# No-operations ahead of VectorE's first operation, and implied waits between an engine's own operations declared away, in a sum of reciprocals

## The chip, the cores and the metric

The kernel runs on one core of one Trainium2 chip. A core has five engines with instruction queues of their own: TensorE (PE in the profile; its weight loads are PEld), VectorE (DVE), ScalarE (ACT), GpSimd (POOL) and SyncE (SP), which here only issues DMAs. Sixteen DMA engines move data between HBM and the on-chip memory SBUF; TensorE writes to a second memory, PSUM, of eight banks. The metric is device time in microseconds (us) on the one core. One execution was profiled; durations and waits below are from it.

## The reference

```python
def setup_inputs():
    batch, seq, dim = 32, 512, 1024
    return {"x": np.abs(np.random.randn(batch, seq, dim)).astype(np.float32) + 1e-6}

def reference(x):
    return np.sum(1.0 / x, axis=-1).astype(np.float32)
```

The input is 32 x 512 rows of 1024 positive float32 numbers, 67.1 MB in all; the output is one sum of reciprocals per row. Nothing is reused, so every byte is read from HBM once.

## The kernel before

**Tiling.** Each of the 128 partitions holds 128 input rows ("row r" is one row in every partition, 128 x 1024 numbers). Rows arrive in `ring`, 40 row slots in SBUF. The last two rows are worked in two halves each, so they appear in the plan as 126 to 129.

**Arithmetic.** With a row's halves a and b, 1/a + 1/b = (a + b) / (a b). The product a*b is made by POOL (step P, line 199) or, for some rows, by DVE (V with one half copied into PSUM by a TensorE step C, line 209; W straight from SBUF; both line 220). ACT turns products into reciprocals in two passes, Ln (step L, line 242) and Exp with scale -1 (step E, line 251), usually two rows at once, in the `prod` slots or into PSUM. For some rows PE adds the halves into PSUM (step S, line 232, two matmuls with the identity `ident`). DVE ends every row with one multiply-and-accumulate (step R, line 267): over the whole row times the reciprocal, or over the added halves times the reciprocal. The profile shows it as a CUSTOM operation and a short READ_ACCUMULATOR that writes `sums`. A row's ring slot is free again after its last reader.

**Order of the work.** Nothing is scheduled automatically. `PLAN` is a list of tokens written out by hand (`P18`, `L16+2@18`, `R15`, `D9`); the loop over `ops` emits one instruction after the other, and each engine runs its own in that order. A `D` token issues the next loads on SP's DMA queue: 33 loads, first of 2, 10, 14 and 14 rows, later smaller, at the end one row and then half a row each. The results leave in six parts after the rows below 114 are done (line 289) and one at the end (line 291).

**Waits.** The framework puts a semaphore wait wherever an instruction touches a region that another one touched, unless it has already waited for a later instruction of that engine. `note` (line 135) keeps a history of who touched which ring half, `prod` slot or PSUM bank; for each operation of another engine that a wait already made is known to cover, it declares that there is no dependence, and the framework leaves the wait out. Pairs on the same engine are skipped by `if o_engine == engine: continue` (line 147), so for them the framework's waits stay. In the instruction list of this kernel that leaves 77 waits of ACT on its own semaphore, 21 of DVE and 17 of POOL. An instruction carries one wait; a further one becomes an instruction of its own ahead of it (EVENT_SEMAPHORE in the trace, not counted as busy): DVE has 45 of those among its 332 instructions, POOL 39.

Of the kernel before, what the change touches and what calls it, by code (L numbers as in the profile page):

```python
# [11 lines left out]
def kernel(  # L12
# [5 lines left out]
    nc = tc.nc  # L18
# [5 lines left out]
    R = 40  # L24
    NP = 22
    LAST = F - 2
    DONE = 114
    S = float(2**17)

    PLAN = """
        D2 D10 D14 D14 P0+2 C3@3 S2@0 V3 P2 L0+2@0 C11@3 S3@1 E0+2@6 P4+2 V11 L2+2@2 R0 S6@2
        E2+2 R1 P6+2 L4+2@4 R2 R3 E4+2@6 S7@0 P8+2 L6+2@8 R4 S10@1 E6+2 R5 P10 L8+2@10 R6 R7  # L40
        S11@2 E8+2@6 L10+2@6 R8 E10+2 R9 D11 R10 R11 P12+2 C19@3 S14@0 V19 P14+2 L12+2@12
        S15@1 E12+2@6 S18@2 R12 P16+2 L14+2@16 R13 E14+2 R14 P18 L16+2@18 R15 S19@0 E16+2@6
        P20+2 L18+2@14 R16 S22@1 E18+2 R17 D9 P22+2 L20+2@20 R18 R19 E20+2@6 S23@2 P24+2
        L22+2@0 R20 E22+2 R21 L24+2@2 R22 R23 E24+2@6 P26 C27@3 R24 S26@0 P28+2 V27 R25 D7
        L26+2@4 C35@3 E26+2 S27@1 P30+2 V35 L28+2@8 R26 S30@2 R27 E28+2@6 P32+2 L30+2@10 R28
        S31@0 E30+2 R29 P34 L32+2@12 S34@1 R30 R31 E32+2@6 P36+2 S35@0 L34+2@6 R32 E34+2 R33
        D7 P38+2 S38@2 L36+2@16 R34 R35 E36+2@6 S39@1 P40+2 L38+2@18 R36 C43@3 E38+2 R37 D6
        S42@0 P42 L40+2@14 V43 R38 E40+2@6 P44+2 R39 S43@2 L42+2@20 R40 E42+2 S46@1 R41 D3
        P46+2 L44+2@0 R42 R43 E44+2@6 S47@0 P48+2 L46+2@2 R44 S50@2 E46+2 R45 P50 L48+2@4
        R46 C51@3 R47 E48+2@6 S51@1 P52+2 V51 R48 D6 L50+2@8 C59@3 E50+2 R49 P54+2 S54@0  # L50
        L52+2@10 V59 R50 E52+2@6 R51 S55@2 P56+2 L54+2@12 R52 E54+2 S58@1 R53 D5 P58
        L56+2@16 R54 R55 E56+2@6 S59@0 P60+2 L58+2@6 R56 S62@2 E58+2 R57 D4 P62+2 L60+2@14
        R58 R59 E60+2@6 S63@1 P64+2 L62+2@18 R60 S66@0 E62+2 R61 D4 P66 L64+2@20 R62 C67@3
        R63 E64+2@6 P68+2 S67@2 V67 R64 L66+2@0 S70@1 R65 D4 E66+2 P70+2 L68+2@2 R66 R67
        S71@0 E68+2@6 P72+2 L70+2@4 R68 D3 E70+2 R69 D2 C75@3 P74 L72+2@10 S74@2 R70 V75
        P76+2 E72+2@6 R71 S75@1 L74+2@8 R72 D2 E74+2 R73 D2 P80 S78@0 L76+2@12 R74 P81
        L80@16 R75 S79@2 E76+2@6 P78+2 L81@17 R76 D2 S81@1 E80@5 E81 R80 L78+2@6 W82 E78+2
        R81 R77 D1 D1 D1 D1 D1 P88 C85@6 S85@1 R78 P83 L88@18 V85 E88@7 R79 P84 S84@0
        L82+2@14 R88 E82+2@5 P86+2 L84+2@19 R82 D1 E84+2 R83 D1 D1 D1 C90@7 P91 L86+2@0
        S91@2 R85 P93 V90 E86+2@5 R84 P92 S90@1 L90+2@2 R87 L93@21 W89 L92@10 R86 D1 D1 D1  # L60
        D1 E93@7 P94 S97@0 E92@6 R93 E90+2 P97 S94@3 L89@11 R92 E89@7 P95 L97@8 R91 S95@4
        E97 R90 L94+2@4 W96 R97 P101 C99@6 L96@9 R89 E94+2 S100@0 P98 V99 E96@5 L101@12 R95
        P100 S99@1 L98@13 R96 E101@7 L99+2@16 R101 E98@6 P104 C103@5 R94 E99+2 S105@2 R98
        P102 L104@18 V103 E104@7 W105 L102+2@6 R100 P107+2 C106@6 L105@14 R104 E102+2@4
        S108@0 V106 E105 R102 L106+3@19 P109 S107@3 R103 P110 E106+3 R105 S106@4 R99 P111+2
        L109+2@0 R107 S112@1 R108 E109+2@6 R106 L111+2@10 P114 R109 S111@0 E111+2 R110 P113
        L114@15 R111 C115@7 P116 L113@2 R112 E114@6 V115 E113@5 S117@0 P117 R114 L116@3
        L115@8 P118 E116@7 R113 S118@1 E115@6 P119 L117+2@12 R116 E117+2 R115 P120 S120@2
        L119@9 R117 P121 L120@4 S121@3 R118 E119@7 E120 R119 P122 L121@5 S122@0 E121 R120
        P123 L122@18 R121 E122 W124 L123@6 R122 L124@7 W125 S125@1 E123@7 E124@6 R123 P126  # L70
        L125@14 P127 L126@16 S127@0 R124 E125 P128 L127@17 S128@2 E126@7 P129 R125 E127
        S129@3 L128@19 R126 L129@20 E128 R127 E129 R128 R129
    """.split()

    Ln = mybir.ActivationFunctionType.Ln
    Exp = mybir.ActivationFunctionType.Exp
# [36 lines left out]
    def place(r):  # L113
        if r < LAST:
            return r, 0, H
        part, q = divmod(r - LAST, F - LAST)
        return LAST + q, part * H, H // 2
# [6 lines left out]
    left = set(range(DONE))  # L124
    bank, copied, halves, summed = {}, {}, set(), set()

    history = {}
    begun = {}
    count = {}
# [1 line left out]
    def note(engine, inst, reads=(), writes=()):  # L135
        inst = inst.ins
        known = dict(begun.get(engine, {}))
        before = {}
        for spaces, writing in ((reads, False), (writes, True)):
            for space in spaces:  # L140
                for other in history.get(space, ()):
                    if writing or other[3]:
                        before[other[0].name] = other
        needed = sorted(before.values(), key=lambda o: -o[4])
        for other in needed:
            o_inst, o_engine, o_tick, _, _, o_known = other
            if o_engine == engine:
                continue
            if o_tick <= known.get(o_engine, 0):
                tc.declare_no_dep(inst, o_inst, reason="implied by other waits")  # L150
                continue
            for e, t in o_known.items():
                known[e] = max(known.get(e, 0), t)
            known[o_engine] = max(known.get(o_engine, 0), o_tick)
        count[engine] = count.get(engine, 0) + 1
        begun[engine] = known
        entry = (engine, count[engine])
        if engine == "SP":
            entry = (f"load {count[engine]}", 1)
        for spaces, writing in ((reads, False), (writes, True)):  # L160
            for space in spaces:
                history.setdefault(space, []).append(
                    (inst, *entry, writing, sum(count.values()), known)
                )
# [10 lines left out]
    def slots(r, n):  # L175
        return [("slot", pslot[q]) for q in range(r, r + n)]

    with tc.manual_schedule():
        for op, r, n, b in ops:
            p = pslot.get(r)  # L180
# [59 lines left out]
            elif op == "L":  # L240
                pg = prod[:, p : p + n, : place(r)[2]]
                inst = nc.scalar.activation(out=pg, in_=pg, func=Ln, scale=S)  # L242
                note("ACT", inst, writes=slots(r, n))
            elif op == "E":
                pg = prod[:, p : p + n, : place(r)[2]]
                rc = pg
                if b is not None:
                    rc = ps[:, b : b + n, : place(r)[2]]
                    for j in range(n):
                        bank[r + j] = b + j  # L250
                inst = nc.scalar.activation(out=rc, in_=pg, func=Exp, scale=-1.0)  # L251
                if b is None:
                    note("ACT", inst, writes=slots(r, n))
                else:
                    banks = [("bank", b + j) for j in range(n)]
                    note("ACT", inst, slots(r, n), banks)
            elif op == "R":
                q, at, w = place(r)
                other = ps[:, bank[r], :w]
                if r in halves:  # L260
                    row = prod[:, p, :w]
                else:
                    row = ring[:, q % R, at : at + 2 * w]
                    row = row.rearrange("p (h e) -> p h e", h=2)
                    other = other.unsqueeze(1).to_broadcast([P, 2, w])
                total = sums[:, q : q + 1]
                inst = nc.vector.tensor_tensor_reduce(  # L267
                    out=row,
                    in0=row,
                    in1=other,  # L270
                    scale=S,
                    scalar=total if q in summed else 0.0,
                    op0=mult,
                    op1=add,
                    accum_out=total,
                )
                summed.add(q)
                note(
                    "DVE",
                    inst,  # L280
                    [("bank", bank[r])],
                    slots(r, 1) if r in halves else rows(r, 1),
                )

                left.discard(r)
                if not left:
                    for c in range(0, DONE, DONE // 6):
                        part = slice(c, min(c + DONE // 6, DONE))
                        nc.sync.dma_start(out=out_v[:, part], in_=sums[:, part])
                    left.add(-1)  # L290
        nc.sync.dma_start(out=out_v[:, DONE:], in_=sums[:, DONE:])


# [28 lines left out]
```

## Time and profile before

| | |
|---|---|
| time, median of 3 runs | 168.35 us (168.28 to 168.44) |
| the profiled execution: span from first to last instruction | 166.3 us |
| its own device time | not on the page; the median stands 2.05 us above its span |
| busy PE / DVE / ACT / POOL | 132.5 / 128.3 / 132.3 / 128.2 us |
| DMA, mean over the span | 404 GB/s, 67.26 MB |
| first load issued | 0.74 us |
| first operation of DVE | 19.89 us |
| last data operation of DVE starts | 163.95 us |

How to read it: the four computing engines are each busy some 130 of 166 us, so none is full over the whole span; the shares say nothing about a stage. The DMA line of the slices is the mean busy share of the sixteen DMA engines. Queue q1 carries the loads and stores; q8 and q14, marked "instruction", carry the engines' own program code. Waits name the engine or transfer that came last.

### The profile page before, as it was taken

The numbers are of one execution on the slowest core, as the hardware profiler recorded it, in microseconds if no ns is written. First come the engines' busy times: TensorE is split into PE (matmuls) and PEld (weight loads), VectorE is DVE, ScalarE is ACT, GpSimd is POOL, SyncE is SP. The second block draws the span as 40 slices with busy tenths as digits, with TensorE's granted clock in tenths as the row PEclk, the third lists the DMA queues.
The fourth block names the chain that finished last, engine by engine and source line by source line (L and its number), as shares of the span: only waits on it lengthen the run. The fifth ranks groups of instructions, "written<-read, shape, count | busy, mean of one in ns | idle before, by whom it ended". The sixth has DMA issues, their size and how long they took to land.

```text
span 166.3 us, 1348 instructions
## 1 busy us (share of the span) xinstructions
PE 132.5 (80%) x292; PEld 55.2 (33%) x292; DVE 128.3 (77%) x282; ACT 132.3 (80%) x157; POOL 128.2 (77%) x81
## 2 busy tenths in 40 slices
PE   0000799978855999999999999988699979989982
PEld 0000333333312444444343433324234424433351
DVE  0000119885787699898998898989899999999994
ACT  3040073949995899999799999996999999999992
POOL 1500795069995999999999999948977869999860
PEclk9999999999996999999999999999999999999999
DMA  5999999999998989999999999999999999999940
GB/s 189 536 394 394 441 441 441 441 441 441 441 441 349 509 368 446 430 417 438 441 434 434 406 426 446 429 424 424 414 437 437 414 410 428 410 409 410 400 139 4
DMA packets 5768, 67.26 MB, mean 404 GB/s; under 512 B 1536, under 2 KB 1536, under 8 KB 3200
## 3 DMA queue, kind: packets, MB, share of 16 engines
q1 hardware_dynamic: 5760, 67.18, 95.6%
q8 instruction: 2, 0.03, 0.1%
q14 instruction: 6, 0.05, 0.1%
HBM read 67.11 MB, written 0.07 MB: 404 GB/s over the span
## 4 chain that ended last, share of the span: by engine, by line
DMA 57%; PE 18%; ACT 8%; DVE 6%; POOL 6%; issue 3%; SPq 1%; ACTq 0%; POOLq 0%; DVEq 0%
DMA ring<-in_x_dram 57%; PE ps L232 15%; POOL prod L199 6%; ACT prod L242 4%; PE ps L209 3%; ACT ps L251 2%; DVE ring L267 2%; DVE prod L267 2%; ACT prod L251 2%; DVE prod L220 1%; SPq L187 1%; DVE sums L267 0%; ACTq L242 0%; POOLq L199 0%; DVEq L317 0%
## 5 line engine op out<-in xcount | busy, mean ns | idle before, releaser
L199 POOL TENSOR_TENSOR prod<-ring 128x1024 f32<-128x1024 f32 (+2 forms) x75 | 127.5, 1727 | 33.5 <-DMA ring<-in_x_dram 27.1
L232 PE MATMUL ps<-ring,ident 128*128 128x512 f32 (+1 forms) x260 | 116.9, 596 | 5.2 <-DVE sums L267 4.5
L242 ACT ACTIVATE prod<-prod 128x1024 f32<-128x1024 f32 (+2 forms) x78 | 68.5, 892 | 24.9 <-DVE prod L220 14.3
L267 DVE CUSTOM_DVE_ANT_1 ring<-ring,ps 128x1024 f32<-128x1024 f32 (+1 forms) x65 | 76.4, 1208 | 8.9 <-ACT ps L251 8.7
L232 PEld LDWEIGHTS ps<-ring,ident 128*128 128x128 f32 x260 | 49.2, 193 | 71.7 <-issue 51.6
L267 DVE CUSTOM_DVE_ANT_0 prod<-prod,ps 128x512 f32<-128x512 f32 (+1 forms) x63 | 40.9, 677 | 0.4 <-PE ps L232 0.4
L209 PE MATMUL ps<-ring,ident 128*128 128x512 f32 x32 | 19.3, 689 | 25.7 <-DMA ring<-in_x_dram 24.0
L251 ACT ACTIVATE ps<-prod 128x1024 f32<-128x1024 f32 (+2 forms) x41 | 34.1, 838 | 4.5 <-DVE sums L267 3.7
L251 ACT ACTIVATE prod<-prod 128x1024 f32<-128x1024 f32 (+3 forms) x37 | 34.4, 931 | 0.9
L220 DVE TENSOR_TENSOR prod<-ring,ps 128x512 f32<-128x512 f32 x16 | 10.9, 684 | 26.3 <-PE ps L209 26.3
L209 PEld LDWEIGHTS ps<-ring,ident 128*128 128x128 f32 x32 | 6.0, 213 | 36.0 <-issue 21.4
L267 DVE DVE_READ_ACCUMULATOR2_ANT sums<- 128x1 f32 x130 | 10.7, 82 | 0.0
L220 DVE TENSOR_TENSOR prod<-ring 128x512 f32<-128x512 f32 x6 | 4.1, 688 | 0.1
L84 ACT ACT_TABLE_LOAD x1 | 1.3, 1283 | 0.7 <-PEq L306 0.7
L267 DVE CUSTOM_DVE_ANT_0 prod<-prod,ps,sums 128x256 f32<-128x256 f32 x2 | 0.9, 475 | 0.0
masks.py:197 POOL MEMSET ident<- 128x128 f32 x1 | 0.2, 204 | 0.3 <-POOLq L306 0.3
masks.py:199 POOL TENSOR_SCALAR_AFFINE_SELECT ident<-ident 128x128 f32<-128x128 f32 x1 | 0.3, 292 | 0.1
L306 POOL MEMSET const-float32-0.0<- 128x1 f32 x1 | 0.1, 98 | 0.2 <-issue 0.2
L306 POOL MEMSET const-bfloat16-1.0<- 128x1 bf16 x1 | 0.1, 101 | 0.0
L306 POOL MEMSET const-uint8-127<- 128x1 uint8 x1 | 0.1, 101 | 0.0
L306 POOL MEMSET const-float32-1.0<- 128x1 f32 x1 | 0.1, 98 | 0.0
## 6 DMA issues: line engine op xcount, KB each, us to landing
ring<-in_x_dram SPq DMA_DIRECT2D x2, 7168.0 KB, 41.2
ring<-in_x_dram SPq DMA_DIRECT2D x2, 3584.0 KB, 29.3
ring<-in_x_dram SPq DMA_DIRECT2D x2, 3072.0 KB, 31.9
ring<-in_x_dram SPq DMA_DIRECT2D x3, 2048.0 KB, 34.0
ring<-in_x_dram SPq DMA_DIRECT2D x1, 5632.0 KB, 30.3
ring<-in_x_dram SPq DMA_DIRECT2D x5, 1024.0 KB, 31.8
ring<-in_x_dram SPq DMA_DIRECT2D x1, 5120.0 KB, 16.5
ring<-in_x_dram SPq DMA_DIRECT2D x1, 4608.0 KB, 30.7
```

What stands on the lines that cost most here:

```text
L84: nc.scalar.add_instruction(mybir.InstLoadActFuncSet(name=nc.get_next_instruction_name(), act_func_set_id=act_sets.index("natural_log_exp_ ...
L187: inst = nc.sync.dma_start(out=ring[:, a : a + m, at : at + 2 * w], in_=x_v[:, q : q + m, at : at + 2 * w],)
L199: inst = nc.gpsimd.tensor_tensor(out=prod[:, p : p + m, :w], in0=ring[:, a : a + m, at : at + w], in1=ring[:, a : a + m, at + w : at + 2 * w],
L209: inst = nc.tensor.matmul(ps[:, b, : place(r)[2]], lhsT=ident, rhs=xs(r, 1), start=True, stop=True,)
L220: inst = nc.vector.tensor_tensor(out=prod[:, p, :w], in0=xs(r, 0), in1=in1, op=mult)
L232: inst = nc.tensor.matmul(ps[:, b, : place(r)[2]], lhsT=ident, rhs=xs(r, h), start=h == 0, stop=h == 1,)
L242: inst = nc.scalar.activation(out=pg, in_=pg, func=Ln, scale=S)
L251: inst = nc.scalar.activation(out=rc, in_=pg, func=Exp, scale=-1.0)
L267: inst = nc.vector.tensor_tensor_reduce(out=row, in0=row, in1=other, scale=S, scalar=total if q in summed else 0.0, op0=mult, op1=add, acc ...
L306: nc = _bacc.Bacc("TRN2", target_bir_lowering=False, num_devices=1)
```

## The change

Two edits. First, 58 instructions that do nothing are put on VectorE's queue ahead of everything else that the kernel gives it. Second, the test for "same engine" in `note` moves behind the test for "already known": a pair on the same engine is now declared away too when the waits on other engines already imply it; a pair that nothing implies keeps its wait. For this, R also notes its `sums` column. `PLAN` has the same 461 tokens in the same order, only wrapped differently; the new branches `A` and `Z` are not reached by any token, and the stores are issued at the same place.

```diff
+    IDLE = 58
...
         for other in needed:
             o_inst, o_engine, o_tick, _, _, o_known = other
-            if o_engine == engine:
-                continue
             if o_tick <= known.get(o_engine, 0):
                 tc.declare_no_dep(inst, o_inst, reason="implied by other waits")
+                continue
+            if o_engine == engine:
                 continue
...
+    for _ in range(IDLE):
+        nc.vector.nop(hint="idle", nofuse=True)
     with tc.manual_schedule():
...
                 note(
                     "DVE",
                     inst,
                     [("bank", bank[r])],
-                    slots(r, 1) if r in halves else rows(r, 1),
+                    (slots(r, 1) if r in halves else rows(r, 1)) + [("sum", q)],
                 )
-
                 left.discard(r)
-                if not left:
-                    for c in range(0, DONE, DONE // 6):
...
+            if not left:
+                for c in range(0, DONE, DONE // 6):
...
```

More of the change, by code (lines that the diff above doesn't have):

```diff
@@ L40 @@
         E2+2 R1 P6+2 L4+2@4 R2 R3 E4+2@6 S7@0 P8+2 L6+2@8 R4 S10@1 E6+2 R5 P10 L8+2@10 R6 R7
[L41 to L69, printed above, removed]
@@ L70 @@
-        P123 L122@18 R121 E122 W124 L123@6 R122 L124@7 W125 S125@1 E123@7 E124@6 R123 P126
-        L125@14 P127 L126@16 S127@0 R124 E125 P128 L127@17 S128@2 E126@7 P129 R125 E127
-        S129@3 L128@19 R126 L129@20 E128 R127 E129 R128 R129
+        S11@2 E8+2@6 L10+2@6 R8 E10+2 R9 D11 R10 R11 P12+2 C19@3 S14@0 V19 P14+2 L12+2@12 S15@1
+        E12+2@6 S18@2 R12 P16+2 L14+2@16 R13 E14+2 R14 P18 L16+2@18 R15 S19@0 E16+2@6 P20+2
+        L18+2@14 R16 S22@1 E18+2 R17 D9 P22+2 L20+2@20 R18 R19 E20+2@6 S23@2 P24+2 L22+2@0 R20
@@ new lines @@
+        E22+2 R21 L24+2@2 R22 R23 E24+2@6 P26 C27@3 R24 S26@0 P28+2 V27 R25 D7 L26+2@4 C35@3
+        E26+2 S27@1 P30+2 V35 L28+2@8 R26 S30@2 R27 E28+2@6 P32+2 L30+2@10 R28 S31@0 E30+2 R29
+        P34 L32+2@12 S34@1 R30 R31 E32+2@6 P36+2 S35@0 L34+2@6 R32 E34+2 R33 D7 P38+2 S38@2
+        L36+2@16 R34 R35 E36+2@6 S39@1 P40+2 L38+2@18 R36 C43@3 E38+2 R37 D6 S42@0 P42 L40+2@14
+        V43 R38 E40+2@6 P44+2 R39 S43@2 L42+2@20 R40 E42+2 S46@1 R41 D3 P46+2 L44+2@0 R42 R43
+        E44+2@6 S47@0 P48+2 L46+2@2 R44 S50@2 E46+2 R45 P50 L48+2@4 R46 C51@3 R47 E48+2@6 S51@1
@@ new lines @@
+        P52+2 V51 R48 D6 L50+2@8 C59@3 E50+2 R49 P54+2 S54@0 L52+2@10 V59 R50 E52+2@6 R51 S55@2
+        P56+2 L54+2@12 R52 E54+2 S58@1 R53 D5 P58 L56+2@16 R54 R55 E56+2@6 S59@0 P60+2 L58+2@6
+        R56 S62@2 E58+2 R57 D4 P62+2 L60+2@14 R58 R59 E60+2@6 S63@1 P64+2 L62+2@18 R60 S66@0
+        E62+2 R61 D4 P66 L64+2@20 R62 C67@3 R63 E64+2@6 P68+2 S67@2 V67 R64 L66+2@0 S70@1 R65 D4
+        E66+2 P70+2 L68+2@2 R66 R67 S71@0 E68+2@6 P72+2 L70+2@4 R68 D3 E70+2 R69 D2 C75@3 P74
+        L72+2@10 S74@2 R70 V75 P76+2 E72+2@6 R71 S75@1 L74+2@8 R72 D2 E74+2 R73 D2 P80 S78@0
@@ new lines @@
+        L76+2@12 R74 P81 L80@16 R75 S79@2 E76+2@6 P78+2 L81@17 R76 D2 S81@1 E80@5 E81 R80
+        L78+2@6 W82 E78+2 R81 R77 D1 D1 D1 D1 D1 P88 C85@6 S85@1 R78 P83 L88@18 V85 E88@7 R79
+        P84 S84@0 L82+2@14 R88 E82+2@5 P86+2 L84+2@19 R82 D1 E84+2 R83 D1 D1 D1 C90@7 P91
+        L86+2@0 S91@2 R85 P93 V90 E86+2@5 R84 P92 S90@1 L90+2@2 R87 L93@21 W89 L92@10 R86 D1 D1
+        D1 D1 E93@7 P94 S97@0 E92@6 R93 E90+2 P97 S94@3 L89@11 R92 E89@7 P95 L97@8 R91 S95@4 E97
+        R90 L94+2@4 W96 R97 P101 C99@6 L96@9 R89 E94+2 S100@0 P98 V99 E96@5 L101@12 R95 P100
@@ new lines @@
+        S99@1 L98@13 R96 E101@7 L99+2@16 R101 E98@6 P104 C103@5 R94 E99+2 S105@2 R98 P102
+        L104@18 V103 E104@7 W105 L102+2@6 R100 P107+2 C106@6 L105@14 R104 E102+2@4 S108@0 V106
+        E105 R102 L106+3@19 P109 S107@3 R103 P110 E106+3 R105 S106@4 R99 P111+2 L109+2@0 R107
+        S112@1 R108 E109+2@6 R106 L111+2@10 P114 R109 S111@0 E111+2 R110 P113 L114@15 R111
+        C115@7 P116 L113@2 R112 E114@6 V115 E113@5 S117@0 P117 R114 L116@3 L115@8 P118 E116@7
+        R113 S118@1 E115@6 P119 L117+2@12 R116 E117+2 R115 P120 S120@2 L119@9 R117 P121 L120@4
@@ L73 @@
+        S121@3 R118 E119@7 E120 R119 P122 L121@5 S122@0 E121 R120 P123 L122@18 R121 E122 W124
+        L123@6 R122 L124@7 W125 S125@1 E123@7 E124@6 R123 P126 L125@14 P127 L126@16 S127@0 R124
+        E125 P128 L127@17 S128@2 E126@7 P129 R125 E127 S129@3 L128@19 R126 L129@20 E128 R127
+        E129 R128 R129
     """.split()
@@ L256 @@
                     note("ACT", inst, slots(r, n), banks)
+            elif op == "A":
+                q, at, w = place(r)
+                row = ring[:, q % R, at : at + 2 * w]
+                inst = nc.scalar.activation(out=row, in_=row, func=Ln)
+                note("ACT", inst, writes=rows(r, 1))
+            elif op == "Z":
+                q, at, w = place(r)
+                row = ring[:, q % R, at : at + 2 * w]
+                inst = nc.scalar.activation(
+                    out=row,
+                    in_=row,
+                    func=Exp,
+                    scale=-1.0,
+                    accum_out=sums[:, q : q + 1],
+                )
+                summed.add(q)
+                note("ACT", inst, writes=rows(r, 1) + [("sum", q)])
+                left.discard(r)
             elif op == "R":
@@ L281 @@
                     [("bank", bank[r])],
-                    slots(r, 1) if r in halves else rows(r, 1),
+                    (slots(r, 1) if r in halves else rows(r, 1)) + [("sum", q)],
                 )
                 left.discard(r)
-                if not left:
-                    for c in range(0, DONE, DONE // 6):
-                        part = slice(c, min(c + DONE // 6, DONE))
-                        nc.sync.dma_start(out=out_v[:, part], in_=sums[:, part])
-                    left.add(-1)
+            if not left:
+                for c in range(0, DONE, DONE // 6):
+                    part = slice(c, min(c + DONE // 6, DONE))
+                    nc.sync.dma_start(out=out_v[:, part], in_=sums[:, part])
+                left.add(-1)
         nc.sync.dma_start(out=out_v[:, DONE:], in_=sums[:, DONE:])
```

## The prediction

> **What bounds the kernel now.** I read the DMA slices first, since the input is read once; then the stages, the end of the chain, VectorE's list at the end, and last the records of single DMA packets.
>
> ```profile
> DVE  0000119885787699898998898989899999999994
> DMA  5999999999998989999999999999999999999940
> q1 hardware_dynamic: 5760, 67.18, 95.6%
> q8 instruction: 2, 0.03, 0.1%
> q14 instruction: 6, 0.05, 0.1%
> ```
>
> The loads keep the sixteen DMA engines full from the second slice almost to the end. The dips to 8 lie close to the few "instruction" packets, program code fetched through the same engines: by their own records 8192 bytes at 52.4, 78.2, 109.4, 111.2, 157.7 and 163.0 us, and 16384 bytes at 69.6 and 140.8 us.
>
> ```profile
> 147.00:157.00 10.00, 9.97 (x24) 1.00 1.02 407
> 157.00:164.00 7.00, 6.90 (x20) 1.00 0.44 140
> ```
>
> These are windows of DVE alone (busy time, then clock, DMA share, GB/s). From 147 us to its end DVE is full; over 131 to 164 us its gaps add to 0.22 us.
>
> ```profile
> 147.18 10.17 DMA ring<-in_x_dram
> 157.34 0.02 issue
> 157.37 0.38 DVE prod L220
> ...
> 163.63 0.39 DVE prod L267
> ```
>
> ```profile
> 157.37 0.69 DVE L220 TENSOR_TENSOR prod<-ring 128x512 f32<-128x512 f32 x1
> 157.97 0.68 DVE L267 CUSTOM_DVE_ANT_0 prod<-prod,ps 128x512 f32<-128x512 f32 x1
> 158.58 0.08 DVE L267 DVE_READ_ACCUMULATOR2_ANT sums<- 128x1 f32 x1
> 158.69 0.69 DVE L220 TENSOR_TENSOR prod<-ring 128x512 f32<-128x512 f32 x1
> 159.31 1.21 DVE L267 CUSTOM_DVE_ANT_1 ring<-ring,ps 128x1024 f32<-128x1024 f32 x1
> ```
>
> The chain of waits and DVE's timeline meet here: W124 starts at 157.37, just after its row landed at 157.35, and W125 at 158.70, just after 158.68. Behind W125 DVE has no gap to 164.03. So the end is the landing of rows 124 and 125 plus DVE's last 5.3 us.
>
> What sets a landing: a load is complete when all sixteen DMA engines have reported. For row 124 the first reports at 155.36 and the last at 157.35, so the end hangs on the slowest engine, 1.99 us behind; the next two lag 1.79 and 1.68. Following the packets shows where the lag comes from. Up to 51 us the sixteen lie within 0.42 us. The code packet at 52.42 takes 0.31 us, and the data packet behind it on that engine 2.29 instead of 1.67 us: the engine falls back from 0.02 to 0.95. The one at 111.23 hits the same engine again (0.32, then 1.42 instead of 0.77): 1.95. The others hit other engines: 0.70, 0.67 and 0.63 us of lag for 8 KB, 1.5 for 16 KB. Lag is never caught up, since every engine is full.
>
> Whose code is it? At 52.42 DVE has started 62 of its instructions, at 111.23 190: 128 apart, the same DMA engine. At 163.0 it is at 320, again 128 on. I take these three as DVE's, one for each 128 instructions; the third costs nothing now, as the data has landed by 161.3. By the same count SP's 64th instruction falls at 157.4, next to the fetch at 157.7. Against it: ACT passes a boundary 128 behind its fetch at 78.2 near 162 us, and there is one packet for both.
>
> **The no-operations.** Their row is missing. Above: DVE idles up to 19.89 us, so 58 of them are covered up to 0.33 us each; below: the cheapest instruction of DVE's sequencer in the trace, a wait, takes 0.02 us, together 1.2 us. I take zero on the path; the cover is the load in front of step C3, and without it at most 1.2 us would show. But they move every later instruction by 58 places in the code.
>
> **The waits.** By the rule in `note`, 19 of DVE's 21 own waits and 16 of POOL's 17 are implied; ACT keeps its 77 (each E waits for the L just before it), PE has none, SP's loads are unchanged. R128 and R129 keep theirs, on sums just written. Removing them deletes 14 separate wait instructions on DVE; three more DVE waits sat on the operation itself, and the rest shared an instruction with a PE wait. At 0.02 us each the 14 are 0.3 us of sequencer time, beside running operations: consecutive R steps start 1.14 or 0.61 us apart with or without one between. Bounds: zero to the 0.22 us of DVE's gaps behind 131 us. I take zero, since the two gaps next to the end (0.07 and 0.03 us) are waits for landings. On POOL about 0.1 us passes between a separate wait and the operation behind it, but from 147 us its operations start at each row's landing, so this too is zero.
>
> **The code fetches.** Up to place 320, 58 are added and 13 removed. DVE's boundaries come 45 to 58 of the old places sooner: the first at V11 or earlier (24.5 us or before), the second near 88, the third at R109 or R110, at 144.7 to 145.9 us. The third now lies inside the load stream, which runs to 161.3 us. The slowest engine then carries three fetches. Price of the third: above, 0.97 us, its own last fetch; below, 0.63 us, that of 157.7, among small data packets as here; as an extreme zero, if no fetch comes. I take 0.95, the mean of 0.94 and 0.97, as they are of the same engine and queue. W124 and W125 start that much later, less the 0.03 us gap ahead of W125; rows 117 to 123 shift with them and add nothing, since DVE waits once. POOL's boundary moves too (near 118 us), on an engine with a lag of 0.7.
>
> The Trainium skill, "Runtime: NRT & Kernel Launch", section "Instruction fetch mechanics", says that code comes in 16 KiB blocks of 256 instructions and that crossing a boundary is mostly hidden. Here 8 KB come for 128 of DVE's places, and the fetch is hidden from DVE (no gap at 111.23) but not from the data on its DMA engine; by that rule the change would be worth nothing.
>
> **Sum.** The profiled span of 166.3 us becomes 166.3 + 0.95 - 0.03 = 167.2. The three runs' median stands 2.05 above the span, with nothing of the change in that part: 168.35 + 0.92 = 169.27 us. With 0.63 it is 168.95.
>
> **Rivals.** *Same.* Only two fetches of DVE fall into the stream: either none comes for the third boundary (the ACT boundary without a packet speaks for that), or the first comes so early, during the no-operations, that it precedes the first data packet at 1.76 us. The lag is then 1.95 as before: 168.35, within 168.15 and 168.55; the lower end is the 0.18 us to the next engine's lag. For: 58 puts V3 within two places of the first boundary. Against: SP got a fetch with its program nearly over, and 58 at 0.02 us end near 1.9 us.
>
> The page's rule of hidden crossings belongs to this rival.
>
> *Faster.* POOL's own waits pace the end: the chain runs through POOL from 137.18 to 147.18 us, and six of the 16 waits that go lie behind 137. At 0.09 us ("issue" in the chain) that is 0.54 us, 167.8. It decides only if rows 124 and 125 land earlier too, which needs loads that waited for POOL; against it, DMA is full there and DVE has 0.22 us to give, so even then 168.1 is likelier.
>
> *Slower otherwise.* The no-operations cost over 0.33 us each and delay V3 and the first rows: 58 x 0.1 beyond the cover would be 5.8 us, 174.2. No row is near that price.
>
> **Chances.** A third fetch in the stream 0.60; same 0.25; faster 0.12; dear no-operations 0.03. The predicted time is that of the first, 169.27 us, with its own range 168.9 to 169.4. The range 168.05 to 169.45 holds it and the second case and leaves out most of the faster case and the dear no-operations. A measurement tells 0.2%, 0.34 us, from no change: faster 0.12, same 0.25, slower 0.63.
>
> **What would show it.** In the profile after: a DVE code packet near 145 us; the sixteen reports of the last loads spread over 2.9 us instead of 2.0; an idle piece of DVE ahead of W124, released by the DMA; W125 near 159.6 us; R steps 1.14 and 0.61 us apart as before; V3 still at 19.9 us. Wrong if the third packet is missing, if it hits another DMA engine, or if DVE's idle time behind 131 us shrinks.

## The result and the profile after

The changed kernel takes 169.13 us (median of 4 runs, 169.04 to 169.26); in the same comparison the kernel before took 168.39 us. One of its four runs fell into a slower state (172.2 us) and is left out of the ratio; the other three have a median of 168.35 us. The ratio is 1.005, with a 95% interval of 1.0035 to 1.0065: slower by half a per cent. (`PLAN` has 497 tokens, not 461; they are the same, in the same order, in both kernels.) The profiled execution after has a span of 167.5 us and a time of its own of 169.26 us, 1.76 us above the span.

Slices and queues of the page, after:

```profile
DVE  0000019894788888989988989999899999979994
DMA  4989999999999898999999999999999999999920
q1 hardware_dynamic: 5760, 67.18, 94.7%
q8 instruction: 2, 0.03, 0.1%
q14 instruction: 6, 0.05, 0.1%
```

The DMA engines are as full as before, and there are as many code packets. Only their places differ. By the records of single packets the 8192-byte ones start at 8.09, 77.3, 88.9, 122.7, 146.2 and 158.9 us, the 16384-byte ones at 69.9 and 141.2. At 8.09, 88.9 and 146.2 us DVE had started 60, 192 and 319 of its instructions. These are its three fetches, and now all three lie inside the load stream; before, the third came at 163.0, when the data had landed.

The DMA view of the stretch from 145.5 to 147 us, after:

```profile
q1 hardware_dynamic: 156, 0.61, 102.9%
q14 instruction: 1, 0.01, 1.4%
```

In the kernel before the same stretch has data alone:

```profile
q1 hardware_dynamic: 155, 0.60, 99.3%
```

DVE alone, after, in the windows of the end (busy time, count, then clock, DMA share, GB/s):

```profile
131.00:147.00 16.00, 15.91 (x35) 1.00 1.00 414
147.00:157.00 10.00, 9.09 (x20) 1.00 1.02 407
157.00:166.00 9.00, 8.11 (x24) 1.00 0.36 116
```

From 147 to 157 us DVE now misses 0.91 us, where it was full before. DVE's timeline, after:

```profile
148.58 0.08 DVE L275 DVE_READ_ACCUMULATOR2_ANT sums<- 128x1 f32 x1
149.57 0.69 DVE L210 TENSOR_TENSOR prod<-ring,ps 128x512 f32<-128x512 f32 x1 [0.91 <-PE ps L199]
...
158.39 0.08 DVE L275 DVE_READ_ACCUMULATOR2_ANT sums<- 128x1 f32 x1
158.57 0.69 DVE L210 TENSOR_TENSOR prod<-ring 128x512 f32<-128x512 f32 x1
159.18 0.68 DVE L275 CUSTOM_DVE_ANT_0 prod<-prod,ps 128x512 f32<-128x512 f32 x1
159.78 0.08 DVE L275 DVE_READ_ACCUMULATOR2_ANT sums<- 128x1 f32 x1
159.85 0.69 DVE L210 TENSOR_TENSOR prod<-ring 128x512 f32<-128x512 f32 x1
```

The missing time lies in one piece ahead of V115 at 149.57 us. V115 waits for TensorE's step C115, and the timeline of PE says what that waited for, after and then before:

```profile
148.44 1.10 PE L199 MATMUL ps<-ring,ident 128*128 128x512 f32 x2 [1.23 <-DMA ring<-in_x_dram]
```

```profile
147.24 1.10 PE L209 MATMUL ps<-ring,ident 128*128 128x512 f32 x2 [0.26 <-DVE sums L267]
```

So it is a late load: number 19 (counted from 0; it brings rows 115 and 116) landed at 148.30, before at 147.10. W124 starts at 158.57, just after row 124 landed at 158.54 (before 157.34), and W125 follows at 159.85. DVE ends at 165.20, before at 164.03. The chain of waits, after, runs over the loads almost from the middle:

```profile
86.29 32.70 DMA ring<-in_x_dram
119.06 29.25 DMA ring<-in_x_dram
148.38 10.17 DMA ring<-in_x_dram
159.18 0.68 DVE prod L275
159.86 0.68 DVE prod L210
160.55 1.15 DVE ring L275
```

What made load 19 late is seen in the sixteen reports of each load: when the first and the last DMA engine report (us), and how far the third-slowest, second-slowest and slowest lie behind the first.

```text
            before                             after
load   first..last     lag of last three   first..last     lag of last three
  1    17.28.. 17.68   0.24 0.30 0.40      17.19.. 18.52   0.49 0.51 1.32
  6    83.95.. 85.58   0.69 0.94 1.62      83.88.. 85.84   0.93 1.26 1.97
  7    92.46.. 94.08   0.70 0.94 1.62      92.41.. 94.59   0.92 1.95 2.18
 17   140.18..142.12   0.74 1.65 1.94     140.15..142.35   0.90 1.98 2.21
 18   142.66..144.60   1.65 1.72 1.94     142.62..144.83   1.78 1.98 2.21
 19   145.14..147.10   1.67 1.76 1.96     145.08..148.30   1.82 2.05 3.22
 27   155.36..157.34   1.68 1.80 1.99     155.31..158.54   1.81 2.00 3.23
```

Between loads 18 and 19 of the kernel after, the slowest engine falls back from 2.21 to 3.22 us; the other two stay within 0.07. The code packet of 146.2 us lies in just that interval, and by the records it stands between two data packets of just this engine. From load 19 to load 27 nothing is caught up. Load 27 brings row 124. From load 7 on the first engine reports within 0.06 us of the same time in both kernels, so the 1.20 us by which row 124 lands later is the lag of this one engine.

### The profile page after: what moved, and what is told of

Read it like the earlier page. It is cut to its first block, busy times and chain, and to the rows that moved or that the text cites. A ratio compares the mean times of both kernels' runs of the same rounds, so it can differ in the third digit from the quotient of the medians.

```text
span 167.5 us, 1380 instructions
## 1 busy us (share of the span) xinstructions
PE 131.3 (78%) x292; PEld 54.4 (33%) x292; DVE 128.5 (77%) x282; ACT 132.6 (79%) x157; POOL 128.3 (77%) x81
## 4 chain that ended last, share of the span: by engine, by line
DMA 63%; DVE 14%; ACT 7%; issue 5%; POOL 4%; PE 3%; another core or an unknown queue 2%; SPq 1%; ACTq 0%; DVEq 0%
DMA ring<-in_x_dram 63%; DVE ring L275 8%; POOL prod L189 4%; ACT ps L241 4%; DVE prod L275 4%; ACT prod L232 2%; PE ps L222 2%; DVE prod L210 2%; PE ps L199 1%; ACT prod L241 1%; DVE sums L275 1%; SPq L177 1%; ACTq L232 0%; DVEq L324 0%
## 5 line engine op out<-in xcount | busy, mean ns | idle before, releaser
L189 POOL TENSOR_TENSOR prod<-ring 128x1024 f32<-128x1024 f32 (+2 forms) x75 | 127.6, 1731 | 34.5 <-DMA ring<-in_x_dram 30.7
L222 PEld LDWEIGHTS ps<-ring,ident 128*128 128x128 f32 x260 | 48.7, 192 | 70.9 <-issue 51.4
L199 PE MATMUL ps<-ring,ident 128*128 128x512 f32 x32 | 18.4, 658 | 28.1 <-DMA ring<-in_x_dram 28.0
L199 PEld LDWEIGHTS ps<-ring,ident 128*128 128x128 f32 x32 | 5.7, 205 | 38.8 <-issue 21.3
```

Source lines behind the costliest of these rows:

```text
L189: inst = nc.gpsimd.tensor_tensor(out=prod[:, p : p + m, :w], in0=ring[:, a : a + m, at : at + w], in1=ring[:, a : a + m, at + w : at + 2 * w],
L199: inst = nc.tensor.matmul(ps[:, b, : place(r)[2]], lhsT=ident, rhs=xs(r, 1), start=True, stop=True,)
L222: inst = nc.tensor.matmul(ps[:, b, : place(r)[2]], lhsT=ident, rhs=xs(r, h), start=h == 0, stop=h == 1,)
```

## The experiments

The theory: each code fetch of DVE that falls into the load stream sets the slowest DMA engine back by 0.65 to 1 us (an estimate from the prices before), and the no-operations bring a third one into it. The rivals: the wait edit costs or gains something itself; the no-operations cost time as instructions; anything put ahead on any engine costs as much.

**1. The wait edit alone**

```diff
-    IDLE = 58
+    IDLE = 0
```

> Only the second edit: the implied waits are declared away, no no-operations. Theory (a third code fetch of VectorE inside the load stream costs the time): VectorE's boundaries lie 13 old places later than in the kernel before, its code packets come near 55 and 117 us, the third boundary is past the last load; spread of the reports of the last loads about 2.0 us; 168.4 us, ratio 1.000 within 0.002. Rival (the removed waits change the overlap of the engines and cost the time): 169.1 us, ratio 1.004 or more. Second rival (the removed waits gain and the no-operations lose more): 168.0 us or less.

Measured: 168.39 us, ratio 1.0006 (0.9996 to 1.0016). DVE's fetches come at 52.7 and 116.0 us, and no third one before the loads have landed; the slowest engine is 1.75 us behind. The timeline of DVE in this run:

```profile
157.55 0.69 DVE L210 TENSOR_TENSOR prod<-ring 128x512 f32<-128x512 f32 x1
...
158.86 0.69 DVE L210 TENSOR_TENSOR prod<-ring 128x512 f32<-128x512 f32 x1
```

and its window, full as before the change:

```profile
147.00:157.00 10.00, 9.99 (x24) 1.00 1.02 408
```

It follows that the 14 separate waits taken off DVE (45 become 31) and the 12 off POOL (39 become 27) are worth nothing that can be measured.

**2. The no-operations alone**

```diff
+    for _ in range(58):
+        nc.vector.nop(hint="idle", nofuse=True)
     with tc.manual_schedule():
```

(on the kernel before, whose waits all stay)

> Only the first edit: 58 no-operations ahead of VectorE's first operation, all waits of the kernel before. Theory: the third boundary of VectorE's code falls at old place 262, near 139 us, inside the load stream; three code packets of VectorE, spread of the last reports about 3.0 to 3.2 us, 169.1 us, ratio 1.004 to 1.006. Rival (the removed waits are the cost): 168.4 us.

Measured: 169.10 us, ratio 1.0046 (1.0033 to 1.0058): the whole loss. DVE's fetches come at 8.0, 82.4 and 143.0 us, the slowest engine is 3.22 us behind at row 124. Its window of DVE, and its timeline:

```profile
147.00:157.00 10.00, 9.08 (x20) 1.00 1.03 408
```

```profile
158.44 0.69 DVE L222 TENSOR_TENSOR prod<-ring 128x512 f32<-128x512 f32 x1
...
159.74 0.69 DVE L222 TENSOR_TENSOR prod<-ring 128x512 f32<-128x512 f32 x1
```

The same hole and the same late W124. The third packet came 4 us after the forecast, with 324 instructions started and 143 after the second one, so the count of 128 holds only roughly (121 to 143 between two fetches of DVE, over all kernels but the next). Nothing hung on the difference here.

**3. One fetch more**

```diff
-    IDLE = 58
+    IDLE = 186
```

> Both edits, with 186 instead of 58 no-operations, that is 128 more. At 0.047 us each, as the changed kernel's VectorE list shows, they end near 9.5 us, still ahead of VectorE's first operation at 20 us. Theory: one more block of 128 places is crossed, so four code packets of VectorE lie in the load stream; spread of the last reports near 4.1 us; 0.8 to 1.1 us above the changed kernel, 169.9 to 170.2 us. Rival (the loss comes from where the boundaries fall, which is the same for the last two as with 58, or from a delay of VectorE's first operation, which is not delayed): 169.1 us.

Measured: 170.11 us, ratio 1.0106 (1.0093 to 1.012). There are four fetches of DVE in the stream, at 8.0, 14.9, 89.8 and 147.1 us; the slowest engine is 3.88 us behind at row 124 (4.1 was expected). The first packet comes at 8.0 us as in the changed kernel, where DVE had stood at its 60th instruction since 3.45 us; here it has started 149 by then. So a packet can trail its place in the code by more than 4 us. DVE's timeline of this run:

```profile
159.41 0.69 DVE L210 TENSOR_TENSOR prod<-ring 128x512 f32<-128x512 f32 x1
...
160.63 0.69 DVE L210 TENSOR_TENSOR prod<-ring 128x512 f32<-128x512 f32 x1
```

The fourth fetch costs 0.98 us more by the medians (the third: 0.78 in the changed kernel, 0.83 with the no-operations alone). But this run has 128 more instructions as well, so by itself it does not part the fetches from the instructions. The next one does.

**4. No-operations without a third fetch**

```diff
-    IDLE = 58
+    IDLE = 20
```

> Both edits with 20 no-operations. Theory: the third boundary falls at the R steps of rows 124 to 126, near 161 us, when the last load has landed; two code packets of VectorE in the stream; spread of the last reports 2.0 us; 168.4 us. Rival (each no-operation costs a share): 20/58 of the change's 0.75 us, 168.65 us.

Measured: 168.11 us, ratio 0.9991 (0.9982 to 1.0). The fetches come at 44.5 and 105.7 us, and the third at 161.9, when the last load has landed (161.35). DVE's timeline and window in this run:

```profile
157.40 0.69 DVE L210 TENSOR_TENSOR prod<-ring 128x512 f32<-128x512 f32 x1
...
158.69 0.69 DVE L210 TENSOR_TENSOR prod<-ring 128x512 f32<-128x512 f32 x1
```

```profile
147.00:157.00 10.00, 9.97 (x24) 1.00 1.02 407
```

Twenty no-operations are free. At a fixed price for each, 20 of them would have cost 20/58 of 0.78 us, 0.27 us, that is a ratio of 1.0016; the interval excludes that.

**5. The same no-operations on ScalarE**

```diff
-        nc.vector.nop(hint="idle", nofuse=True)
+        nc.scalar.nop(hint="idle", nofuse=True)
```

> The 58 no-operations stand on ScalarE's queue in place of VectorE's, the waits as in the changed kernel. Theory (only the slowest DMA engine sets a landing): ScalarE's second boundary moves from near 162 us to near 132 us, so ScalarE too has two code packets in the load stream, but on a DMA engine that lags 0.7 to 0.9 us, less than VectorE's 1.75 to 2.0; VectorE's packets come as with the waits alone (52.7 and 116 us). The spread of the last reports stays below 2.1 us and the time at 168.4 us, ratio within 0.002 of 1. Rival (58 no-operations on any engine, or any further code packet in the stream, cost 0.4%): 169.1 us.

Measured: 168.47 us against 168.17, ratio 1.0018 (1.0008 to 1.0027). The packet that had come at 77 to 78 us now comes at 7.9. One comes at 130.0, where ACT has started 197 instructions, and the one that every other kernel has near 158 us (157.7 to 160.1) is missing. The number of code packets within the span is the same as with the waits alone:

```profile
q14 instruction: 5, 0.04, 0.1%
```

So both are ACT's, and its second fetch has moved from behind the landing of row 124 to ahead of it. DVE's stay at 54.2 and 116.7 us. Between loads 13 and 15 the last three lags go from 0.82, 1.75, 2.18 to 1.78, 2.09, 2.21, by this packet and one of 16 KB at 132.4 us: engines that were not the last were set back, the last one was not. DVE has no hole at 149 us:

```profile
147.00:157.00 10.00, 9.98 (x24) 1.00 1.03 408
```

One fetch more ahead of the landing that counts therefore costs little by itself; it costs its full price on the engine that is already last. A small rest (0.30 us by the medians, and the interval lies above 1) is not explained. This trace does not show it: the slowest engine is 2.21 us behind at row 124 and not 1.75 as with the waits alone, but the first one reports earlier, and the row lands at 157.52 us, there at 157.53.

**6. The same no-operations on GpSimd**

```diff
-        nc.vector.nop(hint="idle", nofuse=True)
+        nc.gpsimd.nop(hint="idle", nofuse=True)
```

> The 58 no-operations stand on GpSimd's queue, ahead of its first product, the waits as in the changed kernel. Theory: GpSimd's one code packet in the stream moves from near 123 us to its first operations, before 20 us, and no second one comes before the end, since it has 118 instructions of its own; no change: 168.4 us, ratio within 0.002 of 1. Rival as for ScalarE: 169.1 us. A third possibility: the no-operations end later than 5.66 us, where GpSimd's first product starts, and delay it; that would show as a later first product, hidden behind the second load at 17.7 us.

Measured: 168.43 us against 168.17, ratio 1.0014 (1.0005 to 1.0022). POOL's packet moves from 122.7 to 7.8 us and DVE's stay at 53.0 and 117.8. GpSimd's first product starts at 5.54 us (5.66 before), so it is not delayed. The profiled execution lasted 172.04 us, so its end is not read here. The place of the packets and the time say the same as on ScalarE: the loss belongs to DVE's fetches, not to 58 instructions or an early packet. Here too a rest stays open (0.26 us by the medians).

**7. The third fetch late in the stream**

```diff
-    IDLE = 58
+    IDLE = 40
```

> Both edits with 40 no-operations on VectorE. Theory: the third boundary falls at the V or R steps around 154.5 to 155 us, its packet at 155 to 158 us, between the kernels with 58 (146 us) and with 20 (162 us); the loads of the last rows after it are late by 0.6 to 1.0 us: spread of the reports about 2.0 us for the row before it and 2.6 to 3.0 us for rows 124 or 125; 168.9 to 169.1 us. If the packet comes after 158 us, rows 124 and 125 have landed and the time is 168.3 us. Rival (a share for each no-operation): 168.9 us, but with a spread of 2.0 us.

Measured: 169.14 us, ratio 1.0073 (1.0044 to 1.0102). The fetches come at 34.5, 96.2 and 155.3 us, the first two 26 and 7 us later than in the changed kernel. The last three lags of load 25 are 1.83, 2.03, 2.08, of load 26 they are 1.81, 2.01, 3.04. This time the loads stay in time up to the packet, and the wait shows ahead of W124 itself:

```profile
158.97 0.69 DVE L210 TENSOR_TENSOR prod<-ring 128x512 f32<-128x512 f32 x1 [1.14 <-DMA ring<-in_x_dram]
...
160.22 0.69 DVE L210 TENSOR_TENSOR prod<-ring 128x512 f32<-128x512 f32 x1
```

The profiled execution took 171.24 us, as it lost more behind that point: its granted clock was 0.81 from 157 to 166 us, and at 164.13 DVE had waited 0.91 us for PE. The median did not. All together (the spread is that of load 27, which brings row 124; the execution on GpSimd is not read there):

| kernel | no-operations | DVE's fetches in the stream | spread of row 124's reports, us | W124 starts, us | time, us |
|---|---|---|---|---|---|
| before | 0 | 2 | 1.99 | 157.37 | 168.2 to 168.4 |
| waits alone | 0 | 2 | 1.75 | 157.55 | 168.39 |
| 20 | 20 | 2 | 1.85 | 157.40 | 168.11 |
| on ScalarE | 58 on ACT | 2 | 2.21 | 157.54 | 168.47 |
| on GpSimd | 58 on POOL | 2 | | | 168.43 |
| 40 | 40 | 3 | 3.12 | 158.97 | 169.14 |
| no-operations alone | 58 | 3 | 3.22 | 158.44 | 169.10 |
| after | 58 | 3 | 3.23 | 158.57 | 169.13 |
| 186 | 186 | 4 | 3.88 | 159.41 | 170.11 |

The time goes by the third column and not by the second: 40 and 58 no-operations on DVE cost the same within the intervals, 0 and 20 cost nothing.

## Why the prediction was right

**The time and its cause: right.** 169.27 us was forecast, 169.13 measured, by the mechanism that was given as the likeliest: a third fetch of DVE's code in the load stream, on the DMA engine that sets every landing.

**Price of the third fetch: right in size.** 0.95 us was taken. Load 19 measures 1.01 (2.21 to 3.22), load 26 with 40 no-operations 0.96 (2.08 to 3.04). In the time, where 0.92 was added, it is 0.78 us against the same 168.35, and 0.83 for the no-operations alone. The profiled pair differs by more, 1.2 us of span, because the two executions lie on either side of their medians: at 1.76 us above the span, as after, the profiled execution before comes to 168.06 us, an estimate, some 0.3 below its median.

**End set by rows 124 and 125: right.** W124 starts 0.02 us after its row has landed, in both kernels, and the end moved with it (1.20 and 1.18 us).

**Places of the fetches: two right, one half.** The second was forecast near 88 us and came at 88.9, the third at 144.7 to 145.9 and came at 146.2. The first, "at V11 or earlier", came at 8.09 us, during the wait for V3. That is early enough to have looked like the rival in which the first fetch precedes the data and costs nothing. It did not: the data packet behind it took 2.07 us where the packets there take 1.51, and load 1 already shows the lag of 1.32 us.

**No-operations at zero: right on the path, wrong in detail.** They start 0.047 us apart, not 0.02, and take from 0.76 to 3.45 us, far inside the cover. V3 did not stay at 19.9: it starts at 20.73, not because of the instructions but because the first fetch made load 1 land at 18.52 instead of 17.68. Nothing comes of it, since DVE's loss at the start is not on the chain that ends last.

**Waits at zero: right,** and shown alone (1.0006). R steps are 1.14 to 1.15 or 0.61 us apart as before.

**Spread and idle piece: off.** The spread was forecast at 2.9 and is 3.23: the forecast had the engine begin 0.02 us behind and fall back by 0.93, 1.0 and 0.95; here load 1 would have shown about 0.50 without the packet (the second and third engine stand there), and the three fetches cost 0.82, 0.92 and 1.01, together 3.25. W125 was forecast near 159.6 and came at 159.85. The idle piece was forecast ahead of W124; it lies ahead of V115, because load 19 is the first that the packet delays and DVE needs it through C115. The step that failed is "rows 117 to 123 shift with them and add nothing": it was right on the end, since DVE waits once, but the once is at the first late load that has no work in hand, not at the last. With the fetch at 155.3 (40 no-operations) it is at W124.

**POOL's, ACT's and SP's boundaries.** POOL's was forecast near 118 and came at 122.7. The packet at 157.7 was given to SP. Experiment 5 speaks against that: with the no-operations on ACT it is gone, one comes at 130.0 instead, and SP's instructions are the same. By this one trace it is ACT's second fetch, with 185 of ACT's 203 instructions started. So the prediction's "ACT boundary without a packet" was no ground for the rival, and SP's late fetch none against it; that an engine fetches with its program nearly over still holds, for ACT. No term of the sum hangs on whose packet it was.

**The page's rule.** The Trainium skill, "Runtime: NRT & Kernel Launch", section "Instruction fetch mechanics", has crossings of code blocks mostly hidden. For the engine that fetches, the traces agree: DVE has no gap at 88.9 us, and its hole at 149.57 is a data wait. For the data on the same DMA engine they do not: each crossing of DVE in the changed kernel costs 0.82 to 1.01 us there, and the third one is time of the kernel.

## What to carry to other kernels

Where the DMA engines are full to the end, look at the reports of single DMA engines and not at the mean: a load lands with the slowest of the sixteen, and that one can be last because it also carries code. Count an engine's instructions, no-operations and separate waits included, against the places of the "instruction" packets, and take the count as a rough one; one fetch of 8 KB moved into or out of the stream was worth 0.5% here, whereas 26 waits on work already done were worth nothing. To judge an edit that shifts code, vary the shift alone: 20, 40, 58 and 186 no-operations told the fetch apart from the instructions.

## What the runs showed of the hardware that was not expected

- A no-operation takes DVE 0.047 us from one to the next (0.018 busy), more than twice the 0.02 of a separate wait.
- A code fetch on DVE's DMA engine sets it back by more than the 0.31 to 0.34 us that its packet takes: the data behind it are stretched as well (one packet of 1.725 us instead of about 1.06 behind the one at 88.9, one of 0.968 instead of 0.31 behind the one at 146.2), 0.8 to 1.0 us together, whether the fetch comes at 8, 89, 96, 146 or 155 us.
- The lag stays within 0.06 us from load to load, over 50 us (2.18 at load 7, 2.21 at load 18): here nothing rebalanced the sixteen engines while all were full.
- Which of the "instruction" packets is whose could be read by moving code alone: 58 instructions on ACT took the packet of 77.3 us to 7.9 and that of 158 to 130.0, 58 on POOL that of 122.7 to 7.8.
